# One layer of a hybrid attention encoder on one core: full rows in the value tail, fewer loads for the mixer, sums on DVE, a finer end

## The chip, the core and the metric

The kernel runs on one core of a Trainium2 chip. A core has a matrix engine (TensorE, PE; its weight loads are listed apart as PEld), a vector engine (VectorE, DVE), an activation engine (ScalarE, ACT) and GpSimd (POOL). Each works through its own instructions in a fixed order and waits for the others by semaphores. SyncE (SP) issues most DMA transfers, ACT issues those of the weights. All operands sit in SBUF, 128 partitions wide, and matmul results in PSUM.

The metric is the device time of one execution in microseconds. Before the change three runs gave 2110.64, 2112.69 and 2119.64 us; the median is 2112.69.

## The reference

One layer over two sequences with shared weights, of 1024 and 512 tokens, each with 16 learned meta tokens ahead that are dropped at the end. All values are float32, the model is 1024 wide.

```
n = RMSNorm(h);  [qa|ka|va|qb|kb|vb] = n @ w_in
A: 8 query heads over 2 key heads, q and k normalised and rotated, softmax(q k) v
B: 4 differential heads: (softmax(q0 k0) - lam * softmax(q1 k1)) v, then RMSNorm of the head
h = h + concat(A, B) @ w_out
g = RMSNorm(h) @ w_gate;  g = gelu(conv3 over positions(g) + b)
h = h + (g * (RMSNorm(h) @ w_up)) @ w_down          (2816 wide inside)
y = RMSNorm(h) * g_final, without the meta tokens
```

## The kernel before, in words

Everything is kept transposed: channels on partitions (tiles of 128), tokens along the free dimension. A float32 operand of a matmul is split into a rounded part `hi` (type fp32r, by a cast on ACT) and the rest `lo` (a subtraction on DVE), and each product is three matmuls: hi*hi, hi weight with lo input, lo weight with hi input (`mm3`, L154 to L156; `split`, L147 and L148).

The program has these stages. Projections of both sequences; attention of the short sequence (s = 1) beside projections of the long one (s = 0); attention of the long one beside the short one's mixer and convolutional block, from about 490 to 1303 us; the long one's mixer (to about 1385 us); its gate and up matmuls; and from about 1870 us its down product, `down`, by seven products of quadrants of w_down with sums of quadrants, each in six groups of up to two slices f, and the final norm.

The order of the instructions on each engine is set by a planner when the program is built: it takes the operations in program order with priorities, models their times and interleaves the two sequences. `issue_after` ties an operation behind another in that order. So a change in one operation can move others.

**Attention.** `softmax` makes scores for 128 queries (L532, L533; 1040 keys for s = 0), scales them (L536), and takes exp (L539). `weighted_v` transposes the probabilities p (L553), splits them into pt_hi and pt_lo and multiplies by v (L567, L568 for group A; L563 to L565 for the differential heads). The last 16 keys don't fill a tile of 128. Their slice is taken from the last 32 keys, hi and lo under one another in one tile (64 rows, or 96 for the differential heads), and multiplied in one matmul (L577) by `v_tail`, which `load_v` (L518, L520) brings from a DRAM tensor with zero rows for keys that were already counted. One position of the meta tokens is needed by the convolution; its queries of four heads, two columns each, are gathered in `halo`, 8 queries that pass through the same steps. `diff_block` ends a differential head's block with `o_b`: a copy on ACT (L687), the mean square on PE (L693, L694), three ACT steps (L134, L135, L137), then DVE (L138, L140, L697) and a store to `oT` (L711).

**Mixer.** `mixer_out` loads `oT` back (L774), splits it into xhi and xlo, and multiplies by w_out for eight output tiles j (L154 to L156 into ps_s for the long sequence), adds the residual `res` (L791, L798), stores, and sums squares (L721, L724). The long sequence's columns go in two groups of two pieces of up to 258 columns; group 0 holds columns 0 to 257 and 516 to 773, in the buffer h0 (the trace calls both h), group 1 the others, in h1. k = 0 to 7 numbers the eight tiles of 128 channels; the last differential head writes k = 7, in three blocks of 342 or 341 columns.

**Down and the end.** `combine` makes sums and differences of weight quadrants (L1174, on POOL), `square` sums squares (L1187 on ACT, L1189 on POOL). The second half of the columns of the last product is done as two halves of 256 columns (`half`), so that the first is finished beside the second: `finish` makes the mean of squares on PE (L1199), the root (`rsqrt_newton`, L134 to L140), and `final_norm` (L913 to L918) multiplies by gain and root, eight operations and eight stores for 256 columns.

## Time and profile before

| | before |
|---|---|
| runs, median (lowest to highest) | 2112.69 us (2110.64 to 2119.64), 3 runs |
| profiled execution | 2114.24 us |
| its span, first to last instruction | 2112.5 us |
| mean granted TensorE clock | 0.990 |
| PE busy | 2030.0 us, 96% |
| DVE busy | 1519.7 us, 72% |
| ACT busy | 1019.2 us, 48% |
| POOL busy | 770.0 us, 36% |
| HBM read, written | 189.68 MB, 70.55 MB |

A row of a timeline has the start, the duration, the engine, the line, the operation with output and input, its shape (for a matmul: weight rows*columns, then input rows x columns), a count where neighbours are alike, and in brackets how long the engine had been idle and what ended it. Matmuls overlap: what one costs is the distance to the next one's start. A row of busy time by stretches has the stretch, its length, busy us and instructions of PE, PEld, DVE, ACT and POOL, the granted clock, the DMA share and GB/s.

### The profile page before, as it was taken

How to read it: one execution, taken by the hardware profiler on the slowest of the kernel's cores; microseconds unless marked ns; L12 is line 12 of the kernel's file. 1: busy time of each engine (PE TensorE's matmuls, PEld its weight loads, DVE VectorE, ACT ScalarE, POOL GpSimd, SP SyncE). 2: the span in 40 equal slices, each digit the busy share in tenths (PEclk: the TensorE clock that was granted, in tenths of full speed). 3: DMA queues.
4: the chain of work that ended last, by engine and by line, in shares of the span. 5: the costliest groups of instructions: out<-in, count | busy, mean ns of one | idle time of the engine just before them, and what ended most of it. 6: DMA issues, size and time to landing. Idle time of an engine off the chain costs nothing.

```text
span 2112.5 us, 35876 instructions
## 1 busy us (share of the span) xinstructions
PE 2030.0 (96%) x13734; PEld 1883.5 (89%) x13734; DVE 1519.7 (72%) x2490; ACT 1019.2 (48%) x1885; POOL 770.0 (36%) x609
## 2 busy tenths in 40 slices
PE   8989999997999999999999998999999999999897
PEld 7888989996988888888999997999999999987687
DVE  7756666665677667788878886587767666668986
ACT  6545554555566445445555555455333333344353
POOL 3643344434222121121221122254645444525912
PEclk9999999999999999999999999999999999999999
DMA  5763435546322222323333213763323323256233
GB/s 201 233 224 115 137 108 164 164 131 192 103 66 83 87 73 75 92 80 108 115 97 105 84 57 118 219 169 116 129 85 102 106 85 111 100 196 239 85 105 115
DMA packets 133195, 262.56 MB, mean 124 GB/s; under 512 B 14944, under 2 KB 74400, under 8 KB 132512
## 3 DMA queue, kind: packets, MB, share of 16 engines
q1 hardware_dynamic: 104512, 157.50, 23.2%
q10 hardware_dynamic: 28512, 102.77, 15.5%
q8 instruction: 108, 1.77, 0.3%
q14 instruction: 63, 0.52, 0.1%
HBM read 189.68 MB, written 70.55 MB: 123 GB/s over the span
## 4 chain that ended last, share of the span: by engine, by line
PE 79%; DVE 7%; DMA 4%; POOL 4%; issue 4%; ACT 2%; SPq 0%; DVEq 0%; ACTq 0%; POOLq 0%
PE ps_mm L154 11%; PE ps_mm L155 11%; PE ps_mm L156 11%; PE ps_x L154 6%; PE ps_x L155 6%; PE ps_x L156 6%; PE ps_t L553 6%; PE ps_s L532 4%; PE ps_s L533 4%; PE ps_o L568 2%; PE ps_o L567 2%; POOL a L1174 1%; DVE p L536 1%; PE ps_s L155 1%; PE ps_s L156 1%
## 5 line engine op out<-in xcount | busy, mean ns | idle before, releaser
L155 PE MATMUL ps_mm<-xlo,w_hi 128*128 128x258 f32 (+4 forms) x1352 | 455.5, 337 | 11.6 <-DVE xlo L148 11.6
L154 PE MATMUL ps_mm<-xhi,w_hi 128*128 128x258 f32 (+4 forms) x1352 | 449.3, 338 | 3.0 <-DVE rstd L140 2.3
L156 PE MATMUL ps_mm<-xhi,w_lo 128*128 128x258 f32 (+4 forms) x1352 | 451.6, 334 | 0.0
L536 DVE TENSOR_SCALAR_CACHE_REDUCE p<-ps_s 114x1044 f32<-114x1044 f32 (+5 forms) x212 | 223.3, 1053 | 91.0 <-PE ps_s L533 80.1
L539 ACT ACTIVATE p<-p,nm 114x1040 f32<-114x1040 f32 (+5 forms) x212 | 215.5, 1016 | 150.6 <-DVE p L536 149.5
L155 PEld LDWEIGHTS ps_mm<-xlo,w_hi 128*128 128x128 f32 x1352 | 256.1, 189 | 34.3 <-DVE xlo L148 16.1
L147 ACT CAST pt_hi<-ps_t 128x512 fp32r<-128x512 f32 (+6 forms) x360 | 170.1, 484 | 224.3 <-PE ps_t L553 204.0
L154 PEld LDWEIGHTS ps_mm<-xhi,w_hi 128*128 128x128 f32 x1352 | 256.2, 190 | 23.8 <-DVE rstd L140 2.7
L156 PEld LDWEIGHTS ps_mm<-xhi,w_lo 128*128 128x128 f32 x1352 | 255.9, 189 | 18.3 <-issue 0.7
L148 DVE TENSOR_TENSOR pt_lo<-ps_t,pt_hi 128x512 fp32r<-128x512 f32 (+4 forms) x312 | 172.0, 563 | 105.0 <-ACT pt_hi L147 101.2
L175 POOL CAST w_hi<-w_f 128x1024 fp32r<-128x1024 f32 x66 | 68.1, 1041 | 405.8 <-PE ps_mm L155 189.4
L532 PE MATMUL ps_s<-k,q 128*114 128x348 f32 (+4 forms) x552 | 177.1, 327 | 14.5 <-DVE p L536 14.0
L553 PE MATMUL ps_t<-ident,p 128*128 128x128 f32 (+7 forms) x1188 | 181.5, 268 | 0.0
L533 PE MATMUL ps_s<-k,q 128*114 128x348 f32 (+4 forms) x552 | 170.8, 316 | 0.0
L553 PEld LDWEIGHTS ps_t<-ident,p 128*128 128x128 f32 (+7 forms) x1188 | 140.8, 135 | 30.4 <-issue 5.1
L147 ACT CAST w_hi<-w_f 128x1024 fp32r<-128x1024 f32 x108 | 104.5, 967 | 109.3 <-PE ps_x L155 77.8
L148 DVE TENSOR_TENSOR w_lo<-w_f,w_hi 128x1024 fp32r<-128x1024 f32 (+1 forms) x81 | 114.0, 1408 | 23.5 <-ACT w_hi L147 23.3
L532 PEld LDWEIGHTS ps_s<-k,q 128*128 128x128 f32 (+3 forms) x552 | 100.3, 182 | 23.4 <-DVE p L536 20.6
L147 ACT CAST w_hi<-sums 128x512 fp32r<-128x512 f32 x80 | 47.7, 619 | 130.7 <-PE ps_x L155 116.9
L533 PEld LDWEIGHTS ps_s<-k,q 128*128 128x128 f32 (+3 forms) x552 | 100.5, 182 | 2.5
L154 PE MATMUL ps_p<-xhi,w_hi 128*128 128x256 f32 (+1 forms) x288 | 84.1, 301 | 14.2 <-ACT xhi L273 7.5
L1000 POOL TENSOR_TENSOR sums<-w_f 128x512 f32<-128x512 f32 x40 | 50.8, 1292 | 120.7 <-DVE w_lo L148 118.3
(335 smaller groups left out, 5828.9 us busy)
## 6 DMA issues: line engine op xcount, KB each, us to landing
w_f<-w_gate ACTq DMA_DIRECT2D x46, 512.0 KB
w_f<-w_up ACTq DMA_DIRECT2D x46, 512.0 KB
w_f<-w_in ACTq DMA_DIRECT2D x36, 512.0 KB
w_f<-actT SPq DMA_DIRECT2D x30, 512.0 KB
w_f<-w_out ACTq DMA_DIRECT2D x24, 512.0 KB
w_f<-w_down ACTq DMA_DIRECT2D x22, 512.0 KB
actT<-t SPq DMA_DIRECT2D x11, 1024.0 KB
a<-w_quad ACTq DMA_DIRECT2D x20, 512.0 KB
```

Source lines behind the costliest of these rows:

```text
L147: rounded = nc.scalar.copy(hi, src).ins
L148: rest = (lo_engine or nc.vector).tensor_tensor(out=lo, in0=src, in1=hi.bitcast(F32), op=ALU.subtract).ins
L154: nc.tensor.matmul(ps, lhsT=whi, rhs=xhi, start=start, stop=False)
L155: nc.tensor.matmul(ps, lhsT=whi, rhs=xlo, start=False, stop=False)
L156: g.mark = nc.tensor.matmul(ps, lhsT=wlo, rhs=xhi, start=False, stop=stop).ins
L175: hi_engine.tensor_copy(hi, w)
L532: nc.tensor.matmul(ps[:, i], lhsT=qk[0][0], rhs=qk[0][1][:, kc], start=True, stop=False)
L533: g.scored = nc.tensor.matmul(ps[:, i], lhsT=qk[1][0], rhs=qk[1][1][:, kc], start=False, stop=True).ins
L536: g.evicted = nc.vector.tensor_scalar(out=p.rearrange("p (i w) -> p i w", i=nch), in0=ps, scalar1=-HD ** -0.5, scalar2=3.0e38, op0=ALU.mul ...
L539: nc.scalar.activation(p, p, AF.Exp, bias=nm, scale=-1.0, accum_out=l)
L553: nc.tensor.transpose(tps[:, c:c + M], p[:, k0:k0 + kw], g.ident[:M, :M])
L1000: nc.gpsimd.tensor_tensor(out=out, in0=a, in1=b, op=op)
```

## The change

- In group A's tail the last 64 keys are transposed rather than 32, so that hi and lo fill 128 rows; v_tail for it has 128 rows and a DRAM tensor of its own (`vta`), with more zeros.
- `halo` holds 128 columns, of which the last heads' copies overwrite all but the first 2 i; the product with v uses the first 8 queries.
- In the long sequence's attention the pools for q and p are laid first in memory, then those for small tiles, pt and v.
- `mixer_out` loads several k in one transfer (2, 2, 2, 1, 1), for group 1 four; for group 0 the last k of both pieces comes behind the others. res is not cleared any more; the add covers the real columns alone. Group 1's splits get a high priority.
- `down`: the sums L1174 and L1189 go from POOL to DVE, and are issued behind the splits of a group.
- The end: the last 256 columns are two pieces of 128. The gains are multiplied in early, on ACT or DVE; the root is multiplied in by two DVE operations on four tiles each, with two stores; one of the last piece's stores is issued by ACT.

In `order` rows the line numbers are those of the changed file where it is the change (L523 for L518, L788 for L774, L695 to L705 for L687 to L697, L1145 for L1131, L1189 for L1174, L1204 for L1189).

SP at the start of the long sequence's attention (about 488 to 512 us); v is its first value tile, qk and oT are DRAM tensors. Before:

```order
L332 DMA qk_5_68<-y 128x2x384
L518 DMA v<-v_0_70 128x1024
L520 DMA v_tail<-vt_75 64x128
L448 DMA q<-qk_0_63 128x1x512
L448 DMA q<-qk_0_63 128x1x514
```

and now:

```order
L450 DMA q<-qk_0_63 128x1x512
L450 DMA q<-qk_0_63 128x1x514
L450 DMA q<-qk_0_63 128x1x512
L450 DMA q<-qk_0_63 128x1x514
L334 DMA qk_5_68<-hi 128x2x272 x2
L334 DMA qk_5_68<-y 128x2x272
L719 DMA oT_93<-o_b 128x306
L523 DMA v<-v_0_70 128x1024
L525 DMA v_tail<-vta_76 128x128
L788 DMA h<-oT_93 128x2x513 x3
```

v and v_tail went from ahead of four q loads to behind them, behind three stores of qk and behind the short sequence's last o_b.

ACT at the end of the long sequence's attention (about 1303 to 1316 us); xhi<-h are the mixer's casts, rs_y<-ps_o, rs_y<-rs_y of 342 columns and o_rs belong to the last head's last block. Before:

```order
L689 ACTIVATE o_sq<-o_b 128x342
L147 CAST xhi<-h_15079 128x258
L171 DMA w_f<-w_out 128x1024
L721 ACTIVATE sq<-h 128x256
L134 ACTIVATE rs_y<-ps_o 128x342
L135 ACTIVATE rs_y<-rs_y 128x342
L171 DMA w_f<-w_out 128x1024
L137 ACTIVATE o_rs<-rs_y 128x342
```

and now:

```order
L697 ACTIVATE o_sq<-o_b 128x342
L147 CAST xhi<-h_15072 128x258 x9
L134 ACTIVATE rs_y<-ps_o 128x342
L147 CAST xhi<-h_15072 128x258 x6
L726 ACTIVATE acc<-h 128x256
L134 ACTIVATE rs_y<-ps_mm,eps 128x256
L135 ACTIVATE rs_y<-rs_y 128x342
L135 ACTIVATE rs_y<-rs_y 128x256
L147 CAST w_hi<-w_f 128x1024 x2
L137 ACTIVATE o_rs<-rs_y 128x342
```

The three steps of the last block stood behind one cast; now fifteen casts and two weight casts stand between them. On PE, from the last transposes of p to the first ps_s, 54 matmuls of the short sequence's down product now stand where there were 12. SP issues the last block's store behind all loads of group 0 but one, and then that one, k = 7 of the second piece.

DVE in `down`, in its last product (w_lo<-s is the weight's split, klo what is kept for the last half, h<-ps_mm the adds); L1189 and L1204 stood on POOL before:

```order
L148 TENSOR_TENSOR w_lo<-s_3_21770,w_hi 128x512 x2
L1145 TENSOR_TENSOR h<-ps_mm,h 128x512 x2
L1189 TENSOR_TENSOR a_4_21765<-a_4_21765,a_4_21753 128x512 x2
L148 TENSOR_TENSOR xlo<-w_f,xhi 128x512
L148 TENSOR_TENSOR klo_23040<-a_3_21764,khi_23039 128x1024
L1204 TENSOR_TENSOR acc<-acc,sq 128x512
```

Two sums and one acc came into each such group of the queue.

The diff, cut to what the text speaks of:

```diff
@@ attention
-    sp = pool(ctx, g, f"as{s}", 8, side)
+    sp = pool(ctx, g, f"as{s}", 8, side) if s == 1 else None
     qp = pool(ctx, g, f"aq{s}", 2, side)
-    vp = pool(ctx, g, f"av{s}", 2, side)
+    vp = pool(ctx, g, f"av{s}", 2, side) if s == 1 else None
     pp = pool(ctx, g, f"ap{s}", 9 if s == 0 else 6, side)
+    sp = sp or pool(ctx, g, f"as{s}", 8, side)
     ptp = pool(ctx, g, f"apt{s}", 3 if s == 0 else 2, side)
+    vp = vp or pool(ctx, g, f"av{s}", 2, side)
...
-        tail = vp.tile([P, P], F32R, name="v_tail", tag="v_tail")[:64 if i == 0 else 96]
-        nc.sync.dma_start(out=tail.bitcast(F32), in_=g.vt[s][i][:tail.shape[0], c0:c0 + P])
+        tail = vp.tile([P, P], F32R, name="v_tail", tag="v_tail")[:P if i == 0 else 96]
+        nc.sync.dma_start(out=tail.bitcast(F32), in_=(g.vt[s][i - 1] if i else g.vta[s])[:, c0:c0 + P])
...
-        tps = transposed(n - 32, 32)
+        kt = 32 if diff else 64
+        tps = transposed(n - kt, kt)
         parts = ptp.tile([P, 512], F32R, name="pt_hi", tag="pt_hi")[:, :W]
-        split(g, parts[0:32], parts[32:64], tps)
+        split(g, parts[0:kt], parts[kt:2 * kt], tps)
...
-        halo = sp.tile([P, 8], F32R, name="halo", tag="halo", bufs=2)
+        halo = sp.tile([P, P], F32R, name="halo", tag="halo", bufs=1)
...
-                        nc.vector.tensor_copy(halo[:, 2 * i:2 * i + 2], q[:, :2])
+                        nc.vector.tensor_copy(halo[:, 2 * i:], q[:, :P - 2 * i])
...
-        o, W = yield from weighted_v([p], v, False)
+        o, W = yield from weighted_v([p], v, False, 8)
@@ mixer_out
-                for c0, cw in [(0, C - 1)] if whole else [piece for other in groups for piece in other]:
+                ks = [(0, 2), (2, 4), (4, 6), (6, 7), (7, 8)]
+                loads = [(0, C - 1, ks)] if whole else \
+                    [(*piece, kk) for kk in (ks[:-1], ks[-1:]) for piece in groups[0]] + \
+                    [(*piece, [(0, 4), (4, 8)]) for piece in groups[1]]
+                mix = g.oT[s].rearrange("(k p) c -> p k c", p=P)
+                for c0, cw, ks in loads:
                     cw = min(cw, C - 1 - c0)
-                    for k in range(KT):
+                    for k0, k1 in ks:
                         with tc.issue_after(g.stored) if whole else nullcontext():
-                            load = nc.sync.dma_start(out=st.cols(k, c0, cw),
-                                                     in_=g.oT[s][k * P:(k + 1) * P, c0:c0 + cw]).ins
+                            load = nc.sync.dma_start(out=st.cols(slice(k0, k1), c0, cw),
+                                                     in_=mix[:, k0:k1, c0:c0 + cw]).ins
...
-                        split(g, xhi[k], xlo[k], m)
+                        with tc.high_priority() if group is groups[-1] else nullcontext():
+                            split(g, xhi[k], xlo[k], m)
...
-                    if real < cw:
-                        nc.vector.memset(res[:, real:], 0.0)
...
-                    nc.vector.tensor_tensor(out=hs, in0=ps, in1=res, op=ALU.add)
+                    nc.vector.tensor_tensor(out=hs[:, :real], in0=ps[:, :real], in1=res[:, :real], op=ALU.add)
@@ down
-                nc.gpsimd.tensor_tensor(out=out[n][:, m], in0=a[n][:, m], in1=b[n][:, m], op=op)
+                nc.vector.tensor_tensor(out=out[n][:, m], in0=a[n][:, m], in1=b[n][:, m], op=op)
...
-            nc.gpsimd.tensor_tensor(out=acc, in0=acc, in1=sq, op=ALU.add)
+            nc.vector.tensor_tensor(out=acc, in0=acc, in1=sq, op=ALU.add)
...
+            if behind:
+                with tc.issue_after(rest):
+                    behind(n)
...
-        final_norm(g, op, 0, h[:, :, c0:c0 + cw], rs, c0, cw)
+        y = g.yT[0].rearrange("(k p) c -> p k c", p=P)
+        for k0, queue in ((4, nc.scalar), (0, nc.sync)):
+            part = h[:, k0:k0 + 4, c0:c0 + cw]
+            nc.vector.tensor_tensor(out=part, in0=part, in1=rs[:, None, :].broadcast_to([P, 4, cw]), op=ALU.mult)
+            (queue if c0 + cw == N else nc.sync).dma_start(out=y[:, k0:k0 + 4, c0:c0 + cw], in_=part)
+
+    def gains(ks, c0, cw, engine):
+        for k in ks:
+            gk, hk = g.gain[:, V_GFIN + k:V_GFIN + k + 1], h[:, k, c0:c0 + cw]
+            if engine is nc.scalar:
+                nc.scalar.activation(hk, hk, AF.Copy, scale=gk)
+            else:
+                nc.vector.tensor_scalar(out=hk, in0=hk, scalar1=gk, scalar2=None, op0=ALU.mult)
...
-    product(2, a11, (h12, h22, h21), lambda n: two(n + 1))
-    three(0)
-    product(3, a21, (h22, h21), lambda n: three(n + 1))
+    product(2, a11, (h12, h22, h21), lambda n: (n == 0 and one(end), two(n + 1), n == end and three(0)))
+    product(3, a21, (h22, h21), lambda n: (three(n + 1), n == end and four(0)))
...
-    product(5, s1, (h22, h12), lambda n: (four(n), n and split(g, *keep[n - 1], a12[n - 1])))
+    product(5, s1, (h22, h12), lambda n: (four(n + 1), split(g, *keep[n], a12[n])))
...
+    pieces = [(512, 256), (768, 128), (896, 128)]
...
+    for i, (c0, cw) in enumerate(pieces):
+        before.append(last(c0, cw, beside_last(i)))
+    finish(c0, cw, added(before.pop(), c0, cw))
```

More of the change, by code (lines that the diff above doesn't have):

```diff
@@ L540, in softmax, with weighted_v @@
         return p
-    def weighted_v(pl, v, diff):
-        W = sum(p.shape[0] for p in pl)
+    def weighted_v(pl, v, diff, rows=None):
+        whole = sum(p.shape[0] for p in pl)
+        W = rows or whole
         o = g.psum.tile(P, W, "o")
@@ L1142, in inputs, with product @@
         return load, out
-    def product(i, w, to, before=None, after=None):
+    def product(i, w, to, behind=None, after=None):
         ps = [g.psum.tile(P, 512, "mm") for _ in range(4)]
         for n, grp in enumerate(groups):
-            if before:
-                before(n)
             cols = len(grp) * 512
@@ L1205, in down @@
     product(1, a12, (h11,), after=load(a22, 1, 1))
-    product(4, a22, (h21,), lambda n: n and one(n - 1), load(a21, 0, 1))
-    one(end)
-    two(0)
+    product(4, a22, (h21,), lambda n: (n and one(n - 1), n == end and two(0)), load(a21, 0, 1))
     squares(0, 0, accs[0])
-    product(2, a11, (h12, h22, h21), lambda n: two(n + 1))
-    three(0)
-    product(3, a21, (h22, h21), lambda n: three(n + 1))
+    product(2, a11, (h12, h22, h21), lambda n: (n == 0 and one(end), two(n + 1), n == end and three(0)))
+    product(3, a21, (h22, h21), lambda n: (three(n + 1), n == end and four(0)))
     es.close()
@@ L1217, in down, with last @@
             for n, grp in enumerate(groups)]
-    product(5, s1, (h22, h12), lambda n: (four(n), n and split(g, *keep[n - 1], a12[n - 1])))
+    product(5, s1, (h22, h12), lambda n: (four(n + 1), split(g, *keep[n], a12[n])))
     squares(4, 0, accs[0])
-    split(g, *keep[end], a12[end])
-    def half(c, beside):
-        ps = [g.psum.tile(P, 256, "mm") for _ in range(4)]
+    def last(c0, cw, beside):
+        ps = [g.psum.tile(P, cw, "mm") for _ in range(4)]
+        c, per = c0 - 512, 512 // cw
         for n in range(3):
@@ L1227, in half @@
             beside(n)
-            _, xs = inputs(g.last[c][:, us[0]:us[-1] + 1], len(us) * 256)
+            _, xs = inputs(g.last[c // 256][:, us[0]:us[-1] + 1, c % 256:c % 256 + cw], len(us) * cw)
             for m, f in enumerate(us):
-                x = [part[:, m % 2 * 256:m % 2 * 256 + 256] for part in xs[m // 2]]
+                x = [part[:, m % per * cw:(m % per + 1) * cw] for part in xs[m // per]]
                 grp = (f + 1) // 2
```

73 lines of the change are left out of this document (41 added, 32 removed).

## The prediction

> **What bounds the kernel now.** I read the page first, then the busy time by stretches, then the waits and the order of each engine where TensorE (PE) starts late.
>
> ```profile
> span 2112.5 us, 35876 instructions
> PE 2030.0 (96%) x13734; PEld 1883.5 (89%) x13734; DVE 1519.7 (72%) x2490; ACT 1019.2 (48%) x1885; POOL 770.0 (36%) x609
> ```
>
> PE is the bound nearly everywhere, so only two things count: PE time removed or added, and the few places where PE waits. The profiled execution took 2114.24 us (1.7 us more than its span); the median of the runs is 2112.69, 1.5 us less. I sum against the execution and take 1.5 us off at the end. A measurement of this kernel tells about 0.5% (10.6 us) from no change.
>
> **Full rows and halo.** The starts of neighbouring matmuls give the price of one:
>
> ```profile
> 503.18 0.40 PE L567 MATMUL ps_o<-pt_hi,v 128*128 128x512 f32 x1
> 503.41 0.39 PE L568 MATMUL ps_o<-pt_lo,v 128*128 128x512 f32 x1
> 503.64 0.60 PE L553 MATMUL ps_t<-ident,p 128*128 128x128 f32 x4
> ...
> 525.67 0.50 PE L577 MATMUL ps_o<-pt_hi,v_tail 64*128 64x512 f32 x1
> 526.10 0.66 PE L553 MATMUL ps_t<-ident,p 128*128 128x128 f32 x4
> ...
> 232.01 0.22 PE L553 MATMUL ps_t<-ident,p 8*128 8x8 f32 x1
> 232.16 0.27 PE L568 MATMUL ps_o<-pt_lo,v 128*128 128x8 f32 x1
> ...
> L577 PE MATMUL ps_o<-pt_hi,v_tail x48: 260/447/502, 176.0 to 1302.0; 64*128 64x512 f32 x24, 96*128 96x342 f32 x12, 64*128 64x8 f32 x4, 96*128 96x208 f32 x4
> ```
>
> A tail matmul with 64 rows holds PE for 0.43 us, one of the same width with 128 rows for 0.23. The tile's own row counts 24 of them: 24 x 0.20 = 4.7 us less. The 24 halo transposes go from 8x8 (0.15 us) to 128x128 (four in 526.10 to 526.51, 0.10 each): 1.1 us less. The scores' moving width stays. Wider halo copies and casts run on DVE and ACT while PE has other matmuls; each grows by at most a few tenths. Bounds of this term: 0 (the slowness is not from the rows) to -6.5. I take **-5.8**.
>
> **Start of the long sequence's attention.** One stall goes and one comes.
>
> ```profile
> 488.68 0.34 SPq L518 DMA_DIRECT2D v<-v  x1
> ...
> 489.98 5.45 SPq L448 DMA_DIRECT2D q<-qk  x4
> ...
> 501.28 9.52 DMA oT<-o_b
> ...
> 510.92 0.06 DVE L794 MEMSET res<- 128x1 f32 x1 [5.68 <-DMA oT<-o_b]
> ...
> 511.67 0.55 PE L568 MATMUL ps_o<-pt_lo,v 128*128 128x512 f32 x1 [4.85 <-DVE pt_lo L148]
> ```
>
> The memset waited for a store that took 9.5 us, and the pt_lo behind it on DVE held PE from 506.8 to 511.67. Without the memset this is gone. But v, which was issued ahead of four q loads at 488.68, is now issued behind them and behind that very store. It queues where the store did (landed 510.8), after q loads that start 1.3 us sooner: landed at about 509.5. PE needs v for its first L567, at 503.18 (quoted above), and everything behind that waits; from there to 506.8 are 3.6 us of work, now done by 513.1: **+1.5** against 511.67. If v lands by 506 (the queue is empty sooner), -2; if as late as 513, +5.
>
> **The mixers' input.** PE is busy 12.84 of the 20 us from 1300 here, and waits once more at 1363.9:
>
> ```profile
> 1300.00:1320.00 20.00, 12.84 (x72) 11.39 (x71) 13.81 (x28) 12.93 (x34) 5.86 (x7) 0.74 0.74 218
> ...
> 1301.37 11.29 SPq L774 DMA_DIRECT2D h<-oT  x15
> 1312.76 0.40 SPq L711 DMA_DIRECT2D oT<-o_b  x1
> ...
> 1303.66 1.04 ACT L147 CAST w_hi<-w_f 128x1024 fp32r<-128x1024 f32 x1
> 1307.66 0.49 ACT L137 ACTIVATE o_rs<-rs_y 128x342 f32<-128x342 f32 x1 [0.35 <-ACT rs_y L135]
> 1313.76 3.17 ACT L147 CAST xhi<-h 128x258 fp32r<-128x258 f32 x10
> ...
> 1309.30 0.57 DVE L697 SCALAR_TENSOR_TENSOR o_b<-o_b,gsub,ps_o 128x342 f32<-128x342 f32 x1
> ...
> 1312.33 1.01 PE L154 MATMUL ps_s<-xhi,w_hi 128*128 128x258 f32 x3 [3.36 <-ACT xhi L147]
> ...
> 1357.94 0.42 ACT L721 ACTIVATE sq<-h 128x258 f32<-128x258 f32 x1 [5.65 <-DVE h L798]
> ...
> 1363.90 0.38 PE L154 MATMUL ps_s<-xhi,w_hi 128*128 128x258 f32 x1 [2.67 <-ACT xhi L147]
> ...
> 445.15 2.18 DMA qk<-hi
> ```
>
> The new buffers lie over p, not v. And the order now leaves 54 matmuls of 256 columns behind p's last transposes where it left 12; 42 x 0.12 us (rows below) put these transposes 5 us sooner. So the loads can start near 1295.5 rather than 1301.37, and the first slices are there when PE wants them, at about 1303.6. But PE's first output also needs slice 7 of its second piece, which holds the last head's last block. On ACT, whose order is fixed, that head's three rs steps now stand behind fifteen xhi casts (0.32 each; they end with their loads, near 1307) and its L137 behind two w_hi casts of 1.04: about 1311. DVE then has a w_lo (about 1.2), four norm steps (0.5) and L697: 1314.5 (before 1309.9, stored at 1312.76). Store and load at 2.2 each, a cast and a subtraction: PE goes on near 1320. Before, from 1312.33 at a clock of 0.74, it passed the same matmul at about 1320 too. So the wait moves rather than shrinks; with the clock falling again I take **+1**; bounds -3 (casts bunch and loads are early) and +5.
>
> At 1363.9 PE waited 2.67 us for the second group's first cast, which stands on ACT behind squares that wait for L798, and L798 for its res load in SP's queue, between the other sequence's yT stores. These stores now come sooner in SP's order, and 18 mixer loads are gone from it. But the casts keep their places on ACT, one of them behind a w_hi. Between 0 and -4 (the xlo behind the cast gains too) I take **-2**.
>
> **Down's sums.**
>
> ```profile
> 1940.00:2000.00 60.00, 50.75 (x214) 39.39 (x214) 58.03 (x42) 22.00 (x40) 60.00 (x37) 1.00 0.29 88
> ...
> L155 PE MATMUL ps_mm<-xlo,w_hi 128*128 128x512 f32 x72 | 29.0, 402 | 9.2 <-DVE xlo L148 9.2
> ...
> L148 DVE TENSOR_TENSOR xlo<-w_f,xhi 128x512 fp32r<-128x512 f32 x19 | 29.4, 1574 | 0.1
> ...
> L1174 POOL TENSOR_TENSOR a<-a,a 128x512 f32<-128x512 f32 x18 | 30.8, 1738 | 0.0
> ...
> 1905.84 2.48 DVE L1131 TENSOR_TENSOR h<-ps_mm,h 128x512 f32<-128x512 f32 x4
> ```
>
> While POOL adds, a split on DVE takes 1.57 us; without POOL such an operation takes 0.60 (four in 2.4). PE lost 9.2 us to xlo. The change brings 54 operations to DVE, 54 x 0.60 = 32 us, and takes the stretching away. For this stretch: 42 + 37 operations x 0.60 = 47.4 us beside 50.75 of PE. It fits by a little. The last product is over: a group of two f has two xlo, two w_lo, two sums, two adds, a double klo and an acc, 11 x 0.60 = 6.6 us against 24 matmuls x 0.23 = 5.5. Four such groups are some 4.5 us too long, of which the lead that DVE has built up (two groups of buffers) hides most. I take **-8**; bounds -9.7 and 0.
>
> **The end.** The last 256 columns become twice 128, so 132 matmuls become 264.
>
> ```profile
> 418.56 0.27 PE L563 MATMUL ps_o<-pt_hi,v 128*128 128x208 f32 x1
> 418.67 0.27 PE L564 MATMUL ps_o<-pt_hi,v 128*128 128x208 f32 x1
> 418.78 0.27 PE L565 MATMUL ps_o<-pt_lo,v 128*128 128x208 f32 x1
> ...
> 2090.10 0.28 PE L156 MATMUL ps_mm<-xhi,klo 128*128 128x256 f32 x1
> 2090.22 0.28 PE L154 MATMUL ps_mm<-xhi,khi 128*128 128x256 f32 x1
> ...
> 2098.12 0.59 PE L1199 MATMUL ps_mm<-acc,ones_d 128*128 128x256 f32 x2
> 2099.76 1.41 DVE L1131 TENSOR_TENSOR h<-ps_mm,h 128x256 f32<-128x256 f32 x4
> 2100.67 1.99 PE L1199 MATMUL ps_mm<-sq_p,ones_d 128*128 128x256 f32 x8 [1.96 <-ACT sq_p L1251]
> 2105.10 3.40 DVE L916 SCALAR_TENSOR_TENSOR h<-h,gain,rstd 128x256 f32<-128x256 f32 x6
> ```
>
> At 256 wide one takes 0.12 us, at 512 0.23 (the first rows above): 0.11 per 256 columns, so 0.065 at 128 by width alone. But at 208 wide, where that line gives 0.099, matmuls with a weight change between them take 0.11, as if something else set the pace; I read it as the weights' load, which doesn't shrink with the width. By width: 264 x 0.065 - 132 x 0.12 = +1.4; at the floor: 264 x 0.11 - 15.8 = +13.2. The 208 row is the nearest: +13.2, and +1.1 for the extra sums of squares between the pieces. The tail was 14.4 us from the sums that follow the last product matmul (2098.12) to the span's end. The adds started 1.6 us after that, behind the L916 of the piece before; now they can start about 1.2 us sooner, and at half width take 0.8 for 1.4, the sums 1.1 for 2.0, the root and DVE steps some 1.7 for 2.4, two multiplies of 0.6 each stand for six L916, 2.2 less, with eight stores' issue made two on two queues. By these the tail is about 6 us shorter; the store's own landing stays. 13.2 + 1.1 - 6 = **+8.3**; the lower bound is 1.4 + 1.1 - 6 = -3.5.
>
> The Trainium skill, "TensorE: Matmul & The Clock Gate", § LDWEIGHTS, gives a weight load as columns / 1.2 GHz, 107 ns for 128, close to the 0.11 above, and so speaks against the split. Its § Back-to-back issue gap has 81 ns per matmul at N=128, by which the term would be about +0.7; no run here shows that, and its 131 ns at N=512 is not the 0.23 us of this trace.
>
> **Sum.** -5.8 + 1.5 + 1 - 2 - 8 + 8.3 = -5.0: execution 2109.2, median **2107.7**, within 0.5%.
>
> **Rivals.**
> - Narrow matmuls go by their width (0.065): the end gives -3.5, the sum is -16.8, 2095.9. A pace between this and the floor falls here too (0.08 gives -12.9, 2099.8). For it: 512 and 256 lie on that line; against it the 208 rows.
> - The mixers' stall goes: the last head's store isn't behind the casts in time, PE loses little of the 7 us that it sits idle from 1300 to 1320, and of the slow clock behind them: -9 for +1, sum -15.0, 2097.7. For it: the loads do start sooner. Against it: ACT's order.
> - Slower than before: DVE becomes the bound of down. From the point where its queue falls a group behind (the last product's 6.6 us against 5.5), each further group costs PE the difference, and with ACT's squares and gains waiting on DVE's adds, and its casts behind them, the gain of 8 is lost and some 3 us added (three groups x 1.1): sum +6.0, 2118.7. For it: 47.4 of 50.75 us. Against it: no stretching left.
> - The full rows do nothing, since the 0.43 comes from the form of the last matmul and not from 64 rows: sum +0.8, 2113.5. Against it: 24 rows alike, and the 128-row one beside them.
>
> **Numbers.** Forecast 0.48; narrow by width 0.22; stall gone 0.12; DVE bound 0.13; rows 0.05. The forecast's own range is 2101 to 2114. Faster by over 0.5% (under 2102.1): the first two rivals, 0.30, and 0.03 of the forecast: 0.33. Slower (over 2123.3): part of the third, and v and slice 7 both late: 0.07. Same: 0.60. The range 2094 to 2119 leaves out both faster rivals at once and the worst of the third.
>
> **What would show it.** L577's successors 0.23 us behind it. PE waiting at its first L567 for v, not for pt_lo. PE waiting at slice 7 of ps_s, with L137 behind w_hi on ACT. xlo at about 0.7 us and no PE gap of over 1 us in down. Starts of 128-wide matmuls 0.11 apart; 0.065 would prove the first rival, and a tail of over 10 us or DVE waits in the last product would break my sum.

## The result and the profile after

The changed kernel takes 2101.89 us (median of 6 runs, 2098.38 to 2105.40) against 2113.06 us (6 runs): a ratio of 0.9944, 95% interval 0.9927 to 0.9962. It is faster by 11.2 us between the medians, 0.56% by the ratio. The forecast was 2107.7 us, 5.0 us less, with a range of 2094 to 2119 and "same", within 0.5%, as the likeliest case (0.60). The direction was right and the time lies in the range; but the gain is more than twice the forecast, and the median lies just below 2102.1, in the case "faster", to which the forecast gave 0.33.

The head of the page of the changed kernel:

```profile
span 2100.6 us, 36047 instructions
PE 2033.5 (97%) x13876; PEld 1903.2 (91%) x13876; DVE 1510.8 (72%) x2532; ACT 1027.2 (49%) x1904; POOL 682.8 (33%) x547
```

PE has 142 instructions and 3.5 us of busy time more than before, and the span is 11.9 us shorter, so its idle time fell by 15.4 us. The busy time is a balance: the end adds 14.7 us of matmuls and sums, and most of that is taken off again elsewhere. To see where, I compared the start of the same PE instruction in both traces, stage by stage. The mixer's transition is what PE lost there beyond the usual distance between starts, 20.4 us from 1260 to 1340 against 14.3; the long attention is the rest.

| place (time before) | forecast, us | measured, us |
|---|---|---|
| up to 480 (short attention, projections) | in the rows' term | -4.1 |
| 480 to 520, start of the long attention | +1.5 | +3.0 |
| long attention, 520 to 1290 (full rows) | -5.8 with the above | -9.1 |
| transition to the mixer, 1260 to 1340 | +1 | +6.1 |
| wait at 1363.9 and the xlo behind it | -2 | -6.0 |
| down, with two waits in its last product | -8 | -10.7 |
| the end, pieces and tail | +8.3 | +8.9 |
| sum | -5.0 | -11.9 |

**Full rows.** PE's timeline around one tail of 64 rows before, and around one of 128 rows after:

```profile
763.07 0.32 PE L532 MATMUL ps_s<-k,q 128*128 128x348 f32 x1
763.22 0.32 PE L533 MATMUL ps_s<-k,q 128*128 128x348 f32 x1
763.48 0.50 PE L577 MATMUL ps_o<-pt_hi,v_tail 64*128 64x512 f32 x1
763.90 0.66 PE L553 MATMUL ps_t<-ident,p 128*128 128x128 f32 x4
764.32 0.37 PE L154 MATMUL ps_mm<-xhi,w_hi 128*128 128x258 f32 x1
```

```profile
731.26 0.32 PE L537 MATMUL ps_s<-k,q 128*128 128x348 f32 x1
731.42 0.32 PE L538 MATMUL ps_s<-k,q 128*128 128x348 f32 x1
731.58 0.40 PE L584 MATMUL ps_o<-pt_hi,v_tail 128*128 128x512 f32 x1
731.81 0.60 PE L559 MATMUL ps_t<-ident,p 128*128 128x128 f32 x4
732.17 0.48 PE L154 MATMUL ps_mm<-a_hi,w_hi 128*128 128x512 f32 x1
```

The tail itself falls from 0.42 us to 0.23, as forecast. But the L533 ahead of the old tail held PE for 0.26 us where a 348-wide one takes 0.16 (763.07 to 763.22), and the four transposes behind it took 0.42 us where they take 0.36. Together 0.35 us for this tail, not 0.20; 24 like it would make 8.4 us (run 5 has the sum over all of them).

**Start of the long attention.** PE at its first value product, and SP's queue ahead of it, both after:

```profile
506.82 0.77 PE L573 MATMUL ps_o<-pt_hi,v 128*128 128x512 f32 x1 [5.82 <-DMA v<-v]
```

```profile
495.81 1.13 SPq L719 DMA_DIRECT2D oT<-o_b  x1
496.98 0.42 SPq L523 DMA_DIRECT2D v<-v  x1
```

PE waits 5.8 us for v, which is issued behind the store of o_b, as forecast. That is 1.0 us more than the wait for pt_lo that went; the rest of the 3.0 us goes with a slower clock, 0.83 from 480 to 520 where it had been 1.00 and 0.91.

**Transition to the mixer.** ScalarE, PE, a row of the waits from 1290 to 1325 (us in total, times, longest) and the busy time by stretches, all after:

```profile
1300.67 0.79 ACT L135 ACTIVATE rs_y<-rs_y 128x342 f32<-128x342 f32 x2
1301.35 1.99 ACT L147 CAST w_hi<-w_f 128x1024 fp32r<-128x1024 f32 x2
1303.24 0.49 ACT L137 ACTIVATE o_rs<-rs_y 128x342 f32<-128x342 f32 x1
```

```profile
1313.08 0.58 PE L154 MATMUL ps_s<-xhi,w_hi 128*128 128x258 f32 x1 [3.34 <-ACT xhi L147]
```

```profile
PE ps_mm L154 <- DVE h L889: 3.9, 2, 2.1
```

```profile
1280.00:1300.00 20.00, 16.10 (x121) 15.21 (x120) 11.83 (x31) 10.87 (x32) 4.42 (x6) 0.93 0.55 154
1300.00:1320.00 20.00, 15.57 (x87) 15.01 (x88) 9.17 (x19) 9.11 (x20) 6.67 (x8) 0.71 0.51 139
1340.00:1380.00 40.00, 40.00 (x336) 39.89 (x335) 31.55 (x60) 24.28 (x52) 17.61 (x16) 1.00 0.67 192
```

The root's last step stands behind the two weight casts, and PE waits for slice 7, as forecast, for 3.34 us, as long as it had waited for a cast there (3.36). New are two waits of PE for the short sequence's adds L889, which stand on DVE behind the mixer's splits, 3.9 us together; all waits of this stage make 9.3 us and made 7.2. And the clock is 0.94 and 0.93 in the two stretches from 1260 to 1300, where it had been 1.00; from 1300 to 1320 it is 0.71 and was 0.74. The wait at 1363.9 is gone: PE is busy for all 40 us of its stretch.

**Down.** The stretch from 1940 to 2000, and a group of DVE from 1930 to 2000, after:

```profile
1940.00:2000.00 60.00, 60.00 (x266) 49.68 (x265) 51.39 (x84) 25.76 (x45) 0.00 (x0) 1.00 0.33 101
```

```profile
L148 DVE TENSOR_TENSOR xlo<-w_f,xhi 128x512 fp32r<-128x512 f32 x27 | 18.1, 684 | 2.3 <-ACT xhi L147 2.3
```

A split takes 0.68 us instead of 1.57, PE does not wait in this stretch, and DVE, with twice as many operations, is busy for less time than before. Only in the last product, at 2029 and 2032, PE waits twice for an xlo, which costs some 1.7 us together.

**The end.** Starts of the 128-wide matmuls and the sums behind the last of them, after:

```profile
2089.34 0.28 PE L154 MATMUL ps_mm<-xhi,khi 128*128 128x128 f32 x1
2089.46 0.27 PE L155 MATMUL ps_mm<-xlo,khi 128*128 128x128 f32 x1
2089.57 0.27 PE L156 MATMUL ps_mm<-xhi,klo 128*128 128x128 f32 x1
...
2092.02 0.44 PE L1214 MATMUL ps_mm<-acc,ones_d 128*128 128x128 f32 x2
```

They are 0.11 us apart: 264 of them take 29.6 us, where 132 of 256 columns took 16.0, and 1.1 us of sums come on top. The tail from 2092.02 to the end of the span is 8.6 us, and was 14.4.

### The profile page after: what moved, and what is told of

Its sections match the earlier page's. It is cut to its first block, busy times and chain, and to the rows that moved or that the text cites. A ratio compares the mean times of both kernels' runs of the same rounds, so it can differ in the third digit from the quotient of the medians.

```text
span 2100.6 us, 36047 instructions
## 1 busy us (share of the span) xinstructions
PE 2033.5 (97%) x13876; PEld 1903.2 (91%) x13876; DVE 1510.8 (72%) x2532; ACT 1027.2 (49%) x1904; POOL 682.8 (33%) x547
## 4 chain that ended last, share of the span: by engine, by line
PE 86%; DVE 5%; issue 3%; DMA 2%; ACT 2%; POOL 1%; SPq 0%; DVEq 0%; ACTq 0%; POOLq 0%
PE ps_mm L155 13%; PE ps_mm L154 13%; PE ps_mm L156 13%; PE ps_x L154 6%; PE ps_x L155 6%; PE ps_x L156 6%; PE ps_t L559 5%; PE ps_s L537 4%; PE ps_s L538 4%; PE ps_o L574 2%; PE ps_o L573 2%; PE ps_s L154 2%; PE ps_s L155 2%; PE ps_s L156 2%; PE ps_o L571 1%
## 5 line engine op out<-in xcount | busy, mean ns | idle before, releaser
L154 PE MATMUL ps_mm<-xhi,w_hi 128*128 128x258 f32 (+4 forms) x1352 | 442.8, 336 | 2.5 <-DVE rstd L140 1.8
L541 DVE TENSOR_SCALAR_CACHE_REDUCE p<-ps_s 114x1044 f32<-114x1044 f32 (+4 forms) x212 | 223.1, 1053 | 79.2 <-PE ps_s L538 66.9
L544 ACT ACTIVATE p<-p,nm 114x1040 f32<-114x1040 f32 (+4 forms) x212 | 215.5, 1016 | 129.1 <-DVE p L541 125.6
L559 PE MATMUL ps_t<-ident,p 128*128 128x128 f32 (+6 forms) x1188 | 183.9, 270 | 0.9 <-ACT r_t L603 0.6
L175 POOL CAST w_hi<-w_f 128x1024 fp32r<-128x1024 f32 x66 | 73.5, 1122 | 298.8 <-PE ps_mm L155 163.9
L559 PEld LDWEIGHTS ps_t<-ident,p 128*128 128x128 f32 (+6 forms) x1188 | 145.7, 137 | 26.1 <-issue 1.6
L1043 DVE TENSOR_TENSOR raw_gate<-ps_x,raw_gate 128x516 f32<-128x516 f32 x70 | 47.4, 690 | 59.8 <-PE ps_x L156 59.6
```

The lines of the kernel that those rows point to most:

```text
L154: nc.tensor.matmul(ps, lhsT=whi, rhs=xhi, start=start, stop=False)
L175: hi_engine.tensor_copy(hi, w)
L541: g.evicted = nc.vector.tensor_scalar(out=p.rearrange("p (i w) -> p i w", i=nch), in0=ps, scalar1=-HD ** -0.5, scalar2=3.0e38, op0=ALU.mul ...
L544: nc.scalar.activation(p, p, AF.Exp, bias=nm, scale=-1.0, accum_out=l)
L559: nc.tensor.transpose(tps[:, c:c + M], p[:, k0:k0 + kw], g.ident[:M, :M])
L1043: nc.vector.tensor_tensor(out=out, in0=ps, in1=a, op=ALU.add)
```

## The experiments

Ratios are to the kernel before, run on the same chip (2115.04, 2114.34 and 2114.84 us for runs 1 to 4, 5 to 8 and 9 to 12). A difference to the changed kernel is the difference of the ratios, times 2113 us.

**1. Wide end.** The changed kernel with:

```diff
-    pieces = [(512, 256), (768, 128), (896, 128)]
+    pieces = [(512, 256), (768, 256)]
```

> The changed kernel with its last product in two pieces of 256 columns, as before the change, and everything else of the change kept (early gains, two-operation final norm, sums on DVE). Theory: a 128-column matmul costs the weights' load, 0.11 us, so 264 of them cost 29.6 us and 132 at 0.12 cost 15.8: 13.7 us come back. The tail behind the last product (8.6 us in the changed kernel, 14.4 before) grows by 2.5 to 3.5 us, because the adds, squares, sums and multiplies of the last piece are twice as wide. In sum 10 to 11 us less than the changed kernel: about 2091. Rival: finer pieces pay for themselves, by the shorter tail and by work beside the product; then the time stays within 3 us of the changed kernel, 2099 to 2105.

Measured: 2092.77 us, 0.9897 (0.9879 to 0.9915), 9.9 us less than the changed kernel. Its PE at the last sums:

```profile
2081.87 0.59 PE L1214 MATMUL ps_mm<-acc,ones_d 128*128 128x256 f32 x2
```

With a span of 2094.6 us the tail is 12.7 us: 4.1 us longer, a little more than expected, against some 15 us of matmuls and sums saved. The narrow pieces cost the 0.11 us a matmul of the 208-wide row, and not their width.

**2. Sums on GpSimd again.** The changed kernel with:

```diff
-                nc.vector.tensor_tensor(out=out[n][:, m], in0=a[n][:, m], in1=b[n][:, m], op=op)
+                nc.gpsimd.tensor_tensor(out=out[n][:, m], in0=a[n][:, m], in1=b[n][:, m], op=op)
...
-            nc.vector.tensor_tensor(out=acc, in0=acc, in1=sq, op=ALU.add)
+            nc.gpsimd.tensor_tensor(out=acc, in0=acc, in1=sq, op=ALU.add)
```

> The changed kernel with the weight sums of the down product and the adds of squares back on GpSimd, in the changed order. Theory: GpSimd's adds stretch the splits on DVE to about 1.6 us again and PE waits for xlo: 10 to 13 us more than the changed kernel, about 2113. Rival: the gain came from the order in which the sums are issued (behind the splits of a group), not from the engine: 0 to 3 us more, 2102 to 2105.

Measured: 2116.12 us, 1.0008 (0.9998 to 1.0017), 13.5 us more than the changed kernel. Its splits on DVE from 1930 to 2000, and PE's waits there:

```profile
L148 DVE TENSOR_TENSOR xlo<-w_f,xhi 128x512 fp32r<-128x512 f32 x22 | 32.0, 1483 | 0.0
```

```profile
L155 PE MATMUL ps_mm<-xlo,w_hi 128*128 128x512 f32 x86 | 35.0, 407 | 7.9 <-DVE xlo L148 7.9
```

The stretching is back, and the whole gain of the change is gone with it. By the starts on PE the down product now takes as long as before the change (0.3 us less from 1880 to 2060).

**3. v ahead of p.** The changed kernel with the pool of v laid between those of q and p.

> The changed kernel with the pool of v laid ahead of that of p in the long sequence's attention, small tiles still behind p. The first v is then issued ahead of the q loads again. Theory: PE's wait of 6.1 us for v at its first value product goes, and what remains is the wait for scores; 3 to 5 us less than the changed kernel, 2097 to 2099. The mixer's loads start no later than by 3 us. Rival: with v ahead of p the mixer's buffers lie over something that is free later, its loads start 6 us later and PE waits for them: no gain, 2102 to 2106.

Measured: 2103.35 us, 0.9950 (0.9932 to 0.9969): no gain, as the rival had it. PE's wait for v is gone (in its trace, which is of the slowest of four executions, 2.4 us are won from 480 to 520), and 4.1 us are lost again by 1340. Between the last transposes of p and the mixer's first matmul this trace has no matmul of the short sequence, where the changed kernel has 54; runs 8 and 11 show what that does.

**4. Root first.** The changed kernel with one tie:

```diff
-    nc.scalar.activation(square, y, AF.Square)
+    g.rooted = nc.scalar.activation(square, y, AF.Square).ins
...
         rsqrt_newton(g, op, None, ms, W, None, rs)
+        g.last_root = g.rooted
...
-                        with tc.high_priority() if group is groups[-1] else nullcontext():
+                        late = not whole and group is groups[0] and c0 and 2 <= k < 7
+                        with tc.high_priority() if group is groups[-1] else tc.issue_after(g.last_root) if late else nullcontext():
                             split(g, xhi[k], xlo[k], m)
...
-                w = load_weight(g, g.w_out[j])
+                w = load_weight(g, g.w_out[j], behind=None if whole or group is groups[-1] or j > 1 else g.last_root)
```

Where `behind` is given, `load_weight` puts its split behind that instruction.

> The changed kernel with one tie more on ScalarE: the weight casts of the mixer's first two output tiles and ten of its sixteen input casts stand behind the last head's three steps of the root. Theory: ACT's order held the last head's store back; now its output is stored about 5 us sooner, slice 7 of the second piece is there before PE comes to it, and PE's wait of 3.5 us and the slow clock of about 5 us behind it go: 3 to 6 us less than the changed kernel, 2096 to 2099. Rival: PE then waits for the casts that were put back, or for the adds that stand behind them on DVE, and the sum of the waits between 1295 and 1320 stays: 2101 to 2104.

Measured: 2095.03 us, 0.9909 (0.9893 to 0.9926), 7.4 us less than the changed kernel. Its ScalarE, and its busy time by stretches:

```profile
1290.49 0.43 ACT L134 ACTIVATE rs_y<-ps_o 128x342 f32<-128x342 f32 x1
1290.96 0.49 ACT L135 ACTIVATE rs_y<-rs_y 128x342 f32<-128x342 f32 x1
1291.48 0.49 ACT L137 ACTIVATE o_rs<-rs_y 128x342 f32<-128x342 f32 x1
1291.88 3.17 ACT L147 CAST xhi<-h 128x258 fp32r<-128x258 f32 x10
```

```profile
1300.00:1320.00 20.00, 20.00 (x162) 19.95 (x161) 12.09 (x21) 10.13 (x21) 9.98 (x11) 0.96 0.82 249
```

The three steps stand together, slice 7 comes in time, and PE is busy from 1300 on; what waits are left, 1.8 us for the adds and 2.5 us for w_hi, lie before it. The order of ScalarE was the cause of the wait, and it cost more than the forecast had. The tie moves the splits' subtractions on DVE along with the casts, so the two orders were not tried apart.

**5. Full rows alone**, on the kernel before (v_tail, its tensor and the halo as in the change, nothing else).

> The kernel before with the full rows of the value tail and of the halo alone. Theory: 24 tail matmuls fall from 0.43 to 0.23 or 0.27 us and the halo's transposes by about 1 us in all: 4 to 6 us less than before, a ratio of 0.997 to 0.998. Rival: in the profile of the changed kernel 4 us were gone already at 330 us, where a wait for scores of 3.4 us had become one of 2.8 and the slow clock behind it was gone; if the full rows bring that in every execution, 8 to 10 us less, a ratio of 0.995 to 0.996. Other rival: PE waits elsewhere for what it does sooner, within 2 us of before.

Measured: 2103.57 us, 0.9946 (0.9931 to 0.9961), 11.4 us less than before. The term was sized too small by half; in its trace 24 tails with four neighbours on either side take 35.9 us where they took 43.0. The time is nearer to the first rival than to the theory, but the rival's reason is not needed: run 9 counts what the rows save. In this trace the wait for scores at 321 and the slow clock behind it are 5.0 us cheaper too, and the wait at 1363.9 3.9 us, while 3 us are lost before 150; the first is not so in every run with full rows (last section).

**6. Single loads.** The changed kernel with the mixer's input in eight loads for each piece:

```diff
-                ks = [(0, 2), (2, 4), (4, 6), (6, 7), (7, 8)]
-                loads = ...
+                ks = [(k, k + 1) for k in range(KT)]
+                loads = [(*piece, ks) for piece in ([(0, C - 1)] if whole else [q for other in groups for q in other])]
```

> The changed kernel with the mixer's input loaded by eight transfers for each piece, one per k, in the order of the pieces, as before the change; memory, res and everything else as changed. Theory: the sixteen loads of the second group stand on SP between the other stores and the res loads again, and PE's wait for the second group's first cast (2.7 us at 1363.9 before the change, none now) comes back, with the wait for xlo behind it: 3 to 6 us more than the changed kernel, 2105 to 2109. Rival: it is the earlier start of the loads that took this wait away, by the memory order; within 2 us of the changed kernel, 2100 to 2104.

Measured: 2103.53 us, 0.9948 (0.9933 to 0.9962): the same as the changed kernel. The wait at 1363.9 does not come back, so neither the fewer loads nor their order took it away. The transition looks different at about the same price: one long wait of PE for the sums of squares. The planner moved more than the loads here: 12 matmuls of the short sequence's down product stand behind the last transposes of p, as before the change, and not 54.

```profile
1308.83 1.22 PE L739 MATMUL ps_mm<-acc,ones_d 128*128 128x256 f32 x2 [9.89 <-POOL acc L732]
```

**7. Root first and wide end**, runs 4 and 1 together.

> The changed kernel with two edits together: the root's three steps of the last head ahead of the casts on ScalarE, and the last product in two pieces of 256. Theory: they touch different stages (1290 to 1320 us and the end), so their gains of 7 and 9 us add up: about 2086, a ratio to before of 0.987. Rival: a gain of one is made of the clock's state or is shared; 2090 to 2095.

Measured: 2084.72 us, 0.9858 (0.9842 to 0.9875). The two gains add up (0.9897 + 0.9909 - 0.9944 = 0.9862). It beats both kernels, the changed one by 18 us.

**8. Run 7 with the pool of v behind p**, ahead of the small tiles.

> As the run with root and wide end, with the pool of v laid behind p but ahead of the small tiles in the long sequence's attention. The first v is then issued ahead of the q loads, and the mixer's buffers still lie over p. Theory: PE's wait of 6 us for v goes, the mixer's loads start as early as in the changed kernel: 2 to 5 us less than root and wide, 2081 to 2084. Rival: as with v ahead of p, what is won at 507 us is lost again by 1320 us: within 2 us of root and wide, 2084 to 2088.

Measured: 2096.52 us, 0.9922 (0.9901 to 0.9943), 13.5 us more than run 7 by the ratios, worse than either theory. Its four executions lie between 2093.31 and 2103.84 us, and the trace is of the slowest. PE at the mixer's first matmul:

```profile
1315.69 0.58 PE L154 MATMUL ps_s<-xhi,w_hi 128*128 128x258 f32 x1 [9.74 <-ACT w_hi L147]
```

In PE's order 8 rows stand between the last transposes of p and this matmul, where run 7 has 74; none of them is of the short sequence's down product, where 66 are in run 7. The planner, with v there sooner, had spent the short sequence's matmuls earlier, and PE has nothing left to do while the last head's chain runs.

**9. Tail rows alone**, run 5 without the halo.

> The kernel before with 128 rows in the value tail of group A alone; the halo keeps its 8 queries. Theory: in the trace a tail of 64 rows takes 0.20 us more itself, 0.09 us from the matmul ahead of it and 0.06 us from the one behind; 24 of them are 8.4 us, so three quarters and more of the 10.8 us that the full rows brought: a ratio to before of 0.9955 to 0.9965. Rival: the halo's 8-row transposes, which cost their neighbours too, hold half of it: 0.997 to 0.998.

Measured: 2107.23 us, 0.9965 (0.9954 to 0.9976), 7.4 us less than before. The tails carry most of run 5's gain, and the trace accounts for them: the 24 wide tails with their neighbours take 37.2 us for 43.0, the four of 8 columns 3.7 for 5.5, together 7.5 us less. The halo's share is 4.0 us by the ratios, and the intervals of runs 5 and 9 overlap. The two traces show it, though. One transpose of 8 rows in run 9, and one of 128 in run 5:

```profile
686.12 0.40 PE L571 MATMUL ps_o<-pt_lo,v 128*128 128x512 f32 x1
686.45 0.22 PE L556 MATMUL ps_t<-ident,p 8*128 8x8 f32 x1
686.60 0.43 PE L534 MATMUL ps_s<-k,q 128*128 128x348 f32 x1
686.87 0.32 PE L535 MATMUL ps_s<-k,q 128*128 128x348 f32 x1
```

From the first start to the last these are 0.75 us; in run 5 the same four stand at 687.79, 688.02, 688.05 and 688.30, 0.51 us. 18 such transposes stand between 685 and 945, and run 5 wins 3.9 us on run 9 there.

**10. Sums on DVE alone**, on the kernel before: the edit of run 2 the other way round, in the old order.

> The kernel before with the weight sums of the down product and the adds of squares on VectorE instead of GpSimd, in the old order (ahead of the splits of a group). Theory: what GpSimd's adds cost is the stretching of DVE's splits (1.55 to 1.7 us each for 0.68), so most of the gain of 13 us comes with the engine alone: 9 to 13 us less than before, 0.994 to 0.996. Rival: with the sums ahead of the splits on DVE's own queue, PE waits for the splits instead: 0 to 6 us less.

Measured: 2110.78 us, 0.9984 (0.9975 to 0.9994), 3.4 us less than before: the rival. Its splits on DVE, and PE's waits, from 1930 to 2000:

```profile
L148 DVE TENSOR_TENSOR xlo<-w_f,xhi 128x512 fp32r<-128x512 f32 x23 | 15.5, 682 | 3.8 <-ACT xhi L147 3.8
```

```profile
L155 PE MATMUL ps_mm<-xlo,w_hi 128*128 128x512 f32 x93 | 36.7, 394 | 5.5 <-DVE xlo L148 5.5
```

The stretching is gone, and PE still waits 5.5 us for xlo, since the sums stand ahead of the splits on DVE. With run 2, where the place alone left the down product as long as before: the engine and the place behind the splits are both needed. The place stands here for all that the change reorders in `down`; its parts were not tried apart.

**11. Run 8 with the gap filled**: the planner's share of the short sequence during the long attention lowered.

```diff
-R1, R2, R3 = (1.0, 0.8), (1.0, 0.7), (1.0, 1.0)
+R1, R2, R3 = (1.0, 0.8), (1.0, 0.66), (1.0, 1.0)
```

> As the run with root, wide end and v behind p (2096.5), with the share of the short sequence's work that the planner spends during the attention lowered from 0.7 to 0.66, so that 74 rows of PE's order instead of 8 stand again between the last transposes of p and the mixer's first matmul. Theory: that run lost its gain because early v had moved the other sequence's matmuls out of this gap, and PE had nothing to do for 10 us; with the gap filled the early v shows: 2 to 4 us below root and wide (2084.7), 2080 to 2083. Rival: the memory order holds the mixer's loads back; 2092 to 2097 again.

Measured: 2087.29 us, 0.9870 (0.9855 to 0.9885), 11 us less than run 8: the missing matmuls were the cause of its loss. But it is not below run 7: in its trace it loses 1.1 us on run 7 from 480 to 720, in place of winning, and 3.1 more between 1280 and 1320. At the place where PE had waited for v it now waits for the short sequence's mixer:

```profile
509.71 0.38 PE L154 MATMUL ps_mm<-xhi,w_hi 128*128 128x258 f32 x1 [1.70 <-POOL xhi L798]
511.43 0.39 PE L155 MATMUL ps_mm<-xlo,w_hi 128*128 128x258 f32 x1 [1.34 <-POOL xlo L799]
```

**12. Run 11 with two multiplies of rotation tables on DVE** instead of GpSimd (L437).

> As the run before it, with two multiplies of rotation tables by rstd (128x1040, 2.4 us each) on VectorE instead of GpSimd. Theory: at 315 us a DVE operation on one column took 3.5 to 4.9 us beside GpSimd's multiply, and PE waited 2.4 to 4.3 us for scores behind it, with a slow clock of 5 us behind the longer waits; without it 3 to 6 us less than the run before it, 2076 to 2079. Rival: DVE's own 2.4 us of multiplies hold the scores back as long: within 2 us of it.

Measured: 2101.53 us, 0.9934 (0.9915 to 0.9952), 13.5 us more than run 11. The first multiply on DVE:

```profile
309.73 1.24 DVE L437 TENSOR_TENSOR rope<-rope,rstd 128x1040 f32<-128x1040 f32 x1 [10.59 <-DMA rope<-rope]
```

It waits 10.6 us for its table, and everything behind it on DVE waits along, PE's pt_lo among it. Neither theory had asked when the table lands. The time can't say what the multiply beside DVE costs; the traces can (last section).

## Why the prediction was right, and where not

- **Full rows, -5.8: mechanism right, size wrong.** Measured alone -11.4, outside the bounds I gave (0 to -6.5). A failed step is "a tail matmul with 64 rows holds PE for 0.43 us, one of the same width with 128 rows for 0.23": it took the distance to the next start as the whole price (and 24 x 0.20 is 4.8, not 4.7). The matmul ahead of the tail loses 0.10 us and those behind it 0.06. The halo's 1.1 us failed by the same step: run 5 wins 3.9 us more than run 9 where its transposes stand. The Trainium skill, "TensorEngine Tiling (Array Packing)", § Tiling Modes, Key Properties, says that changing the tiling mode drains the engine; the rows around 763.48 fit that, 0.16 us of them being the neighbours', but no run here shows the mode itself. Tails of 96 rows show nothing of the kind: 342-wide ones stand 0.16 us from their successors.
- **Start of the attention, +1.5.** The wait stands where it was put, for v behind that store. In the trace it cost 3.0 us, with the slow clock; runs 3, 8 and 11 show that an early v gives this back only to lose it elsewhere, so the term is worth little either way.
- **Transition, +1.** The order of ScalarE was read rightly, and run 4 shows it by removing it (-7.4 us). The failed step is "so the wait moves rather than shrinks": the wait for a cast stayed as long as it was, but beside it came two waits for the short sequence's adds, 3.9 us, which I had not followed on DVE, and a slower clock from 1260 to 1300. +6.1 lies outside the bounds (-3 to +5).
- **Wait at 1363.9, -2.** It went whole, 6.0 us with the xlo behind it and a clock of 0.50 for 3.4 us, outside the bounds (0 to -4). I gave two reasons; run 6 refutes the 18 fewer loads. The other, that the other sequence's stores end sooner, was not tried alone, nor were the missing memset, the memory order and the high priority of group 1's splits. Part of it needs none of them: in the traces of runs 5, 9 and 10, whose mixer is the one before, the wait for the cast is 0, 0.9 and 1.0 us instead of 2.7, while the 1.3 to 1.4 us for the xlo stay. So some of the gain here may be no work of the change, and its cause stays open.
- **Down, -8.** Measured -10.7 in the trace, and 13.5 us by taking it back (run 2). The step "54 x 0.60" fits (0.68 each, with starts 0.60 apart). But I told it as a gain of the engine alone; run 10 shows that 3.4 us are, and the rest needs the sums behind the splits. The forecast overflow of the last product did come, 1.7 us. -10.7 lies outside the bounds (-9.7 to 0).
- **The end, +8.3.** Measured +8.9: matmuls 13.6 for the forecast 13.2, sums 1.1, tail -5.8 for -6. The step from the 208-wide row to the floor was right, and the first rival is refuted by starts 0.11 apart and by run 1. The 81 ns a matmul at 128 columns that the Trainium skill has ("TensorE: Matmul & The Clock Gate", § Back-to-back issue gap) do not show here.
- **The rivals.** That the mixer's stall goes, that DVE becomes the bound and that the rows do nothing did not happen. That the rows do nothing was the case I should have turned round: "they do more" was missing.

Four of the six terms lie outside their own bounds, and the sum came out within the range by luck, because errors of both signs stand in it: gains too small by 5.6 us (rows, by run 5), 4.0 (wait at 1363.9) and 2.7 (down), losses too small by 5.1 (transition), 1.5 (start) and 0.6 (end).

## What to carry to other kernels

Price an odd instruction by the stretch around it, from two starts ahead to two behind, not by the distance to the next start: nearly half the cost of a partial-row matmul lay in its neighbours (0.16 of 0.35 us). When work moves to a busier engine, its place in that engine's order decides as much as its duration: the same sums were worth 13.5 us behind the splits and 3.4 us ahead of them, and a multiply that waited for a load blocked a whole queue for 10 us. Where two streams are interleaved, what covers a chain at a stage's end is the other stream's remaining work; an earlier operand can spend that cover.

## What the runs showed of the hardware

**The clock makes a wait cost up to twice its length, and not every time.** Busy time by stretches around the wait for scores at 321 (its row stands first), before and then after; the clock is the third number from the end of a row:

```profile
321.04 0.55 PE L532 MATMUL ps_s<-k,q 128*102 128x264 f32 x1 [3.24 <-DVE p L536]
```

```profile
317.00:321.00 4.00, 0.80 (x7) 0.67 (x6) 3.96 (x5) 1.26 (x3) 4.00 (x4) 0.98 0.83 236
321.00:328.00 7.00, 6.96 (x27) 6.61 (x28) 3.78 (x13) 2.90 (x9) 3.49 (x3) 0.52 0.75 212
```

```profile
316.00:320.00 4.00, 1.52 (x13) 1.30 (x12) 3.93 (x6) 0.42 (x3) 3.34 (x3) 1.00 0.85 215
320.00:327.00 7.00, 7.00 (x53) 6.97 (x54) 5.22 (x16) 4.26 (x13) 3.42 (x3) 1.00 0.70 208
```

After 3.24 us of idling PE ran at 0.52 for 7 us, after 2.5 us at full speed: 3 us of the 4 that were won by 480. Over all traces but run 12's the two starts there are 2.2 to 4.3 us apart, in no order of the changes, so that part of the gain belongs to the execution that was profiled more than to the change. The Trainium skill, "TensorE: Matmul & The Clock Gate", § Part 1, has the clock halved after an idle window of about 3.4 us whose start is free of the program; these two rows fit that. But shorter waits came with a slow clock too: behind a single wait of 2.19 us at 1439.9 it was 0.50 for 3.4 us, before and after alike. And not always: with nearly the same four waits from 480 to 500 (0.83, 1.35, 1.4 and 1.35 us) it was 1.00 before and 0.83 after.

```profile
480.00:500.00 20.00, 15.05 (x99) 13.66 (x99) 12.36 (x22) 10.60 (x18) 6.38 (x4) 1.00 0.55 172
```

```profile
480.00:500.00 20.00, 15.05 (x85) 13.29 (x84) 12.72 (x23) 11.65 (x20) 5.56 (x4) 0.83 0.69 215
```

**A one-column operation on DVE waits until GpSimd's two-input operation ends.** It is what the wait at 321 waits for. DVE, then GpSimd, before:

```profile
315.00 4.56 DVE L679 SCALAR_TENSOR_TENSOR c<-l_b,r_b,neglam 104x1 f32<-104x1 f32 x1
```

```profile
317.16 2.38 POOL L434 TENSOR_TENSOR rope<-rope,rstd 128x1040 f32<-128x1040 f32 x1
```

It ends with that multiply, the last of three operations with two input tensors that GpSimd does without a pause from 314.61 on. The same operation stands 56 times in this trace; the first row has its shortest, median and longest time in ns, the others one more such pair:

```profile
L679 DVE SCALAR_TENSOR_TENSOR c<-l_b,r_b,neglam x56: 207/220/4561, 308.1 to 1261.1; 114x1 f32<-114x1 f32 x36, 102x1 f32<-102x1 f32 x12, 104x1 f32<-104x1 f32 x8
354.81 1.46 DVE L679 SCALAR_TENSOR_TENSOR c<-l_b,r_b,neglam 104x1 f32<-104x1 f32 x1
353.88 2.38 POOL L148 TENSOR_TENSOR w_lo<-w_f,w_hi 128x1024 fp32r<-128x1024 f32 x1
```

All six that took more than 0.3 us began beside such an operation of GpSimd and ended within 0.02 us of its end, as these two rows do (356.27 and 356.26). In run 12, without the multiplies on GpSimd, the one at this place took 0.22 us. The Trainium skill, "SBUF — State Buffer", § Who interferes with whom, says that a DVE instruction with two SBUF inputs contends with a GpSimd instruction that reads SBUF. The rows agree, and so do the splits (1.48 us beside GpSimd's sums in run 2, 0.68 without).
